# A column mean over 8192 rows: the last row group of the last 64 KB load is summed by TensorE instead of VectorE, and the accumulator is summed ahead of the last two row groups

## The chip, the cores and the metric

The kernel runs on one core of one Trainium2 chip. The metric is the device time of one execution in microseconds (us). Runs of one batch were made on one chip, with the kernel before timed beside them. The "span" is the profiled part of an execution and is some 1.8 us shorter than its time (631.2 us against 633.02 us in the profiled run of the kernel before). In profile lines PE is TensorE's matmuls and PEld its weight loads, DVE is VectorE, ACT ScalarE, POOL GpSimd and SP SyncE; a "q" behind the name is that engine's own queue, issuing a transfer. The "granted clock" is the share of TensorE's full clock that the records of a run show.

## The reference

```
x: 8192 x 8192 float32
out = np.mean(x, axis=0)         # 8192 float32
```

The input is 268.4 MB, so this is a kernel of loads. Row group g is the 128 rows from 128g on, one row for each partition; there are 64 of them, 0 to 63. (In a load of two row groups the rows are dealt out two to a partition, which a sum does not notice.)

## The kernel before

VectorE adds row groups into an accumulator of 128 x 8192, which leaves one row for each partition. TensorE then sums over the partitions, by matmuls with a stationary operand of 1/8192. The sums stand in PSUM tiles: four "banks" and a small one, the "edge". The last two row groups are given to TensorE straight, so that they need no add on VectorE.

```python
def sums(row, blocks, first, last):      # sum over partitions, into PSUM
    for i in blocks:
        if i < NBLK:                     # 15 blocks of 512 columns, four to a bank,
            mm(banks[i // 4], i % 4, row[:, i * F:(i + 1) * F], first, last)   # one column tile each
        else:                            # block 15: four short sums, the "edge"
            for q in range(4):
                c = i * F + q * W
                mm(edge, q, row[:, c:c + W], first, last)
# ... loads of 64 KB (two row groups) or 32 KB (one) per partition; for each row group:
            elif g < G - 3:
                nc.vector.tensor_add(out=acc[:], in0=acc[:], in1=row)
            else:                        # row group 61: in four chunks
                for c in range(0, N, 4 * F):
                    s = slice(c, c + 4 * F)
                    nc.vector.tensor_add(out=acc[:, s], in0=acc[:, s], in1=row[:, s])
# ... row group 62 in one load, row group 63 in pieces of 8, 4, 3 and 1 blocks
    cuts = [(0, 8), (8, 12), (12, 15), (15, 16)]
# ...
    sums(t[:, 0, :], range(NBLK + 1), True, False)       # row group 62
    for b in range(4):
        sums(acc, range(4 * b, 4 * b + 4), False, False) # accumulator
    for lo, hi in cuts:
        sums(t[:, 1, :], range(lo, hi), False, True)     # row group 63
        # for each bank now complete:
        #   nc.scalar.copy(out=r[:32 * n, :], in_=banks[b][:32 * n, :])
        #   nc.scalar.dma_start(out=o, in_=r[0:32 * n:32, :])
        # for the edge: copy by VectorE, store by SyncE
```

The scheduler that places these instructions may move them on an engine where no dependence forbids it.

Of the kernel before, what the change touches and what calls it, by code (L numbers as in the profile page):

```python
# [1 line left out]

# [4 lines left out]


@with_exitstack
def kernel(  # L10
    ctx: ExitStack,
    tc: tile.TileContext,
    x: bass.AP,
    out: bass.AP,
):










    nc = tc.nc
    f32 = mybir.dt.float32
    M, N = x.shape
    P = nc.NUM_PARTITIONS
    F = 512  # L30
    W = F // 4
    NBLK = N // F - 1
    G = M // P

    pairs = ctx.enter_context(tc.tile_pool(name="pairs", bufs=2))
    singles = ctx.enter_context(tc.tile_pool(name="singles", bufs=1))
    sg = ctx.enter_context(tc.tile_pool(name="sg", bufs=1))
    psp = ctx.enter_context(tc.tile_pool(name="psum", bufs=1, space=bass.MemoryType.PSUM))
    resp = ctx.enter_context(tc.tile_pool(name="res", bufs=1))

    acc = sg.tile([P, N], f32, name="acc")
    ones = sg.tile([P, 32], f32, name="ones")
    warm = sg.tile([P, 32], f32, name="warm")
    nc.gpsimd.memset(ones[:], 1.0 / M)  # L44
    nc.scalar.copy(out=warm[:], in_=ones[:])  # L45
    banks = [psp.tile([P, F], f32, name=f"bank{b}") for b in range(4)]
    edge = psp.tile([P, W], f32, name="edge")

    def mm(dst, q, rhs, first, last):
        nc.tensor.matmul(  # L50
            out=dst[32 * q:32 * q + 32, :],
            lhsT=ones[:],
            rhs=rhs,
            start=first,
            stop=last,
            tile_position=(0, 32 * q),
            skip_group_check=True,
        )

    def sums(row, blocks, first, last):  # L60
        for i in blocks:
            if i < NBLK:
                mm(banks[i // 4], i % 4, row[:, i * F:(i + 1) * F], first, last)
            else:
# [4 lines that stand above are left out]
    g = 0  # L69
    k = 0  # L70
    prev = None
    while g < G - 2:
        n = 1 if k % 3 == 2 and g + 2 < G - 2 else 2
        if n == 2:
            t = pairs.tile([P, 2, N], f32, name="pair")
            src = x[g * P:(g + 2) * P, :].rearrange("(p j) c -> p j c", j=2)
            nc.sync.dma_start(out=t[:], in_=src)  # L77
            rows = [t[:, 0, :], t[:, 1, :]]
        else:
            t = singles.tile([P, N], f32, name="single")  # L80
            nc.sync.dma_start(out=t[:], in_=x[g * P:(g + 1) * P, :])
            rows = [t[:]]
        for row in rows:
            if g == 0:
                prev = row
            elif g == 1:
                nc.vector.tensor_add(out=acc[:], in0=prev, in1=row)  # L87
            elif g < G - 3:
                nc.vector.tensor_add(out=acc[:], in0=acc[:], in1=row)  # L89
            else:  # L90
                for c in range(0, N, 4 * F):
                    s = slice(c, c + 4 * F)
                    nc.vector.tensor_add(out=acc[:, s], in0=acc[:, s], in1=row[:, s])  # L93
            g += 1
        k += 1

    t = pairs.tile([P, 2, N], f32, name="pair")
    nc.sync.dma_start(out=t[:, 0, :], in_=x[g * P:(g + 1) * P, :])
    cuts = [(0, 8), (8, 12), (12, 15), (15, 16)]
    for lo, hi in cuts:  # L100
        cs = slice(lo * F, hi * F)
        nc.sync.dma_start(out=t[:, 1, cs], in_=x[(g + 1) * P:(g + 2) * P, cs])
    sums(t[:, 0, :], range(NBLK + 1), True, False)
    for b in range(4):
        sums(acc, range(4 * b, 4 * b + 4), False, False)
    for lo, hi in cuts:
        sums(t[:, 1, :], range(lo, hi), False, True)
        if hi <= NBLK:
            for b in range(lo // 4, (hi + 3) // 4):
                n = min(hi - 4 * b, 4)  # L110
                r = resp.tile([P, F], f32, name=f"r{b}")
                nc.scalar.copy(out=r[:32 * n, :], in_=banks[b][:32 * n, :])  # L112
                o = out[b * 4 * F:(b * 4 + n) * F].rearrange("(q c) -> q c", q=n)
                nc.scalar.dma_start(out=o, in_=r[0:32 * n:32, :])  # L114
        else:
            r = resp.tile([P, W], f32, name="redge")
            nc.vector.tensor_copy(out=r[:], in_=edge[:])  # L117
            o = out[lo * F:hi * F].rearrange("(q c) -> q c", q=4)
            nc.sync.dma_start(out=o, in_=r[0:P:32, :])


# [1 line left out]
_INS = ['x']  # L123
_OUTS = [((8192,), 'float32')]


# [23 lines left out]
```

## Time and profile before

| | kernel before |
|---|---|
| time, median of the first three runs | 633.48 us (633.03 to 633.92) |
| span of the profiled run | 631.2 us |
| load queue's share of the 16 DMA engines | 98.6% |
| VectorE busy | 530.7 us, 84% |
| TensorE, matmuls | 12.9 us, all behind 614.2 us |

Such a table is read from its largest share: loads fill the span, and only what lies behind the last byte can be moved. The prediction shows the lines for that.

### The profile page before, as it was taken

Reading aid. Unit: us, or ns where it says so; the run is one execution under the profiler, and the core shown is the slowest. Engines: PE = TensorE matmul, PEld = TensorE weight load, DVE = VectorE, ACT = ScalarE, POOL = GpSimd, SP = SyncE. Lnnn points to the kernel's source line nnn. Section 1 sums busy time; section 2 is a strip of 40 time slices with the busy share of each in tenths; the row PEclk is TensorE's granted clock in tenths of the full one; section 3 lists DMA queues with packets and bytes.
Section 4 is the critical chain, followed back from the end, with each engine's and each line's share of the span. In section 5 each row is a group of like instructions: output and inputs, shape, how many; then the busy total and the mean of one; then the engine's idle time right before and its main releaser. Section 6 shows DMA issues by size and latency. Waiting matters only on the chain.

```text
span 631.2 us, 470 instructions
## 1 busy us (share of the span) xinstructions
PE 12.9 (2%) x114; PEld 4.9 (1%) x114; DVE 530.7 (84%) x65; ACT 3.7 (1%) x6; POOL 0.3 (0%) x5
## 2 busy tenths in 40 slices
PE   0000000000000000000000000000000000000007
PEld 0000000000000000000000000000000000000002
DVE  0539889889889889889899898898988988988984
ACT  0000000000000000000000000000000000000001
POOL 0000000000000000000000000000000000000000
PEclk9999999999999999999999999999999999999999
DMA  9999999999999999999999999999999999999994
GB/s 399 424 417 455 432 413 451 440 411 461 415 428 436 465 399 465 399 432 432 465 399 465 399 465 399 466 407 457 415 449 428 436 440 424 449 415 457 407 413 189
DMA packets 6090, 268.50 MB, mean 425 GB/s; under 512 B 692, under 2 KB 696, under 8 KB 967
## 3 DMA queue, kind: packets, MB, share of 16 engines
q1 hardware_dynamic: 6056, 268.44, 98.6%
q10 hardware_dynamic: 30, 0.03, 0.0%
q8 instruction: 1, 0.02, 0.0%
q14 instruction: 3, 0.02, 0.0%
HBM read 268.44 MB, written 0.03 MB: 425 GB/s over the span
## 4 chain that ended last, share of the span: by engine, by line
DMA 64%; DVE 33%; PE 2%; issue 0%; ACT 0%; ACTq 0%; SPq 0%; DVEq 0%
DMA pair<-in_x_dram 64%; DVE acc L89 33%; PE bank L50 2%; ACT r L112 0%; ACTq L114 0%; PE edge L50 0%; SPq L77 0%; DVEq L89 0%
## 5 line engine op out<-in xcount | busy, mean ns | idle before, releaser
L89 DVE TENSOR_TENSOR acc<-acc,pair 128x8192 f32<-128x8192 f32 x47 | 408.5, 8692 | 68.5 <-DMA pair<-in_x_dram 67.8
L89 DVE TENSOR_TENSOR acc<-acc,single 128x8192 f32<-128x8192 f32 x12 | 104.3, 8692 | 0.4
L87 DVE TENSOR_TENSOR acc<-pair 128x8192 f32<-128x8192 f32 x1 | 8.7, 8692 | 22.7 <-DMA pair<-in_x_dram 22.7
L50 PE MATMUL bank<-pair,ones 128*32 128x512 f32 x60 | 9.1, 715 | 614.2 <-DMA pair<-in_x_dram 614.2
L93 DVE TENSOR_TENSOR acc<-acc,pair 128x2048 f32<-128x2048 f32 x4 | 8.9, 2287 | 0.0
L50 PEld LDWEIGHTS bank<-pair,ones 128*32 128x32 f32 x60 | 2.8, 127 | 618.7 <-issue 617.9
L112 ACT COPY r<-bank 128x512 f32<-128x512 f32 (+1 forms) x4 | 2.2, 586 | 624.0 <-PE bank L50 623.3
L117 DVE COPY redge<-edge 128x128 f32<-128x128 f32 x1 | 0.3, 292 | 5.1 <-PE bank L50 5.1
L50 PE MATMUL bank<-acc,ones 128*32 128x512 f32 x30 | 3.8, 595 | 0.0
L50 PE MATMUL edge<-pair,ones 128*32 128x128 f32 x16 | 1.6, 276 | 0.0
L50 PEld LDWEIGHTS bank<-acc,ones 128*32 128x32 f32 x30 | 1.4, 109 | 1.5 <-DVE acc L93 0.7
L45 ACT ACT_TABLE_LOAD x1 | 1.3, 1283 | 0.7 <-PEq L134 0.7
L50 PE MATMUL edge<-acc,ones 128*32 128x128 f32 x8 | 0.8, 276 | 0.0
L50 PEld LDWEIGHTS edge<-pair,ones 128*32 128x32 f32 x16 | 0.8, 109 | 1.1 <-issue 1.1
L50 PEld LDWEIGHTS edge<-acc,ones 128*32 128x32 f32 x8 | 0.4, 109 | 0.6 <-issue 0.6
L45 ACT COPY warm<-ones 128x32 f32<-128x32 f32 x1 | 0.2, 218 | 0.0
L44 POOL MEMSET ones<- 128x32 f32 x1 | 0.1, 124 | 0.3 <-POOLq L134 0.3
L134 POOL MEMSET const-bfloat16-1.0<- 128x1 bf16 x1 | 0.1, 101 | 0.0
L134 POOL MEMSET const-uint8-127<- 128x1 uint8 x1 | 0.1, 101 | 0.0
L134 POOL MEMSET const-float32-0.0<- 128x1 f32 x1 | 0.1, 98 | 0.2 <-issue 0.2
L134 POOL MEMSET const-float32-1.0<- 128x1 f32 x1 | 0.1, 98 | 0.0
## 6 DMA issues: line engine op xcount, KB each, us to landing
single<-in_x_dram SPq DMA_DIRECT2D x12, 4096.0 KB, 31.9
pair<-in_x_dram SPq DMA_DIRECT2D x1, 4096.0 KB
pair<-in_x_dram SPq DMA_DIRECT2D x1, 2048.0 KB
pair<-in_x_dram SPq DMA_DIRECT2D x1, 1024.0 KB, 27.8
pair<-in_x_dram SPq DMA_DIRECT2D x1, 768.0 KB, 29.2
pair<-in_x_dram SPq DMA_DIRECT2D x25, 30.9
pair<-in_x_dram SPq DMA_DIRECT2D x1, 256.0 KB, 29.3
out_dram<-r ACTq DMA_DIRECT2D x3, 8.0 KB
```

The source lines that it names most:

```text
L44: nc.gpsimd.memset(ones[:], 1.0 / M)
L45: nc.scalar.copy(out=warm[:], in_=ones[:])
L50: nc.tensor.matmul(out=dst[32 * q:32 * q + 32, :], lhsT=ones[:], rhs=rhs, start=first, stop=last, tile_position=(0, 32 * q), skip_group_ch ...
L87: nc.vector.tensor_add(out=acc[:], in0=prev, in1=row)
L89: nc.vector.tensor_add(out=acc[:], in0=acc[:], in1=row)
L93: nc.vector.tensor_add(out=acc[:, s], in0=acc[:, s], in1=row[:, s])
L112: nc.scalar.copy(out=r[:32 * n, :], in_=banks[b][:32 * n, :])
L117: nc.vector.tensor_copy(out=r[:], in_=edge[:])
L134: nc = _bacc.Bacc("TRN2", target_bir_lowering=False, num_devices=1)
```

## The change

The intent: VectorE is freed of row group 61's four chunked adds, TensorE has that work early, while VectorE still adds row group 60, and the accumulator, which is then ready sooner, is summed before row group 62, so that less is left to sum when row group 63 lands.

```diff
             elif g < G - 3:
                 nc.vector.tensor_add(out=acc[:], in0=acc[:], in1=row)
             else:
-                for c in range(0, N, 4 * F):
-                    s = slice(c, c + 4 * F)
-                    nc.vector.tensor_add(out=acc[:, s], in0=acc[:, s], in1=row[:, s])
+                sums(row, range(NBLK + 1), True, False)
@@
-    sums(t[:, 0, :], range(NBLK + 1), True, False)
-    for b in range(4):
-        sums(acc, range(4 * b, 4 * b + 4), False, False)
+    sums(acc, range(NBLK + 1), False, False)
+    sums(t[:, 0, :], range(NBLK + 1), False, False)
```

## The prediction

> **What bounds the kernel now.** I read the page's totals first, then the chain of waits, then the end of the run in order of time. The totals:
>
> ```profile
> PE 12.9 (2%) x114; PEld 4.9 (1%) x114; DVE 530.7 (84%) x65; ACT 3.7 (1%) x6; POOL 0.3 (0%) x5
> ...
> q1 hardware_dynamic: 6056, 268.44, 98.6%
> HBM read 268.44 MB, written 0.03 MB: 425 GB/s over the span
> ...
> L93 DVE TENSOR_TENSOR acc<-acc,pair 128x2048 f32<-128x2048 f32 x4 | 8.9, 2287 | 0.0
> ```
>
> The load queue keeps the 16 DMA engines busy for 98.6% of the span. VectorE, at 84%, has slack: a pair of row groups takes about 19.5 us to arrive and 2 x 8.69 us to add. So the body, up to the last byte, is bound by the loads, and the change touches no load. Work taken off VectorE is worth nothing by itself. What can be gained lies behind the last byte, and I look for the chain there:
>
> ```profile
> 592.82 21.25 DMA pair<-in_x_dram
> 614.06 0.14 issue
> 614.20 4.59 PE bank L50 x25
> ...
> 619.72 2.74 PE bank L50 x24
> ...
> 623.40 0.91 PE bank L50 x4
> 624.31 0.02 issue
> 624.33 0.59 ACT r L112
> 624.92 0.02 issue
> 624.95 1.11 ACTq L114
> ...
> 627.88 0.58 ACT r L112
> ```
>
> The first column is the start in us. Row group 62 lands at 614.06. From then on TensorE never waits: row group 62, the accumulator, row group 63. Bank 0 is complete at 624.31, and then ScalarE runs its four copies and four store issues one behind another; the span ends at 631.2, 6.87 us after the first copy starts. In the stretches of time the loads die away before that: 0.99 of the DMA engines busy up to 622.5, 0.19 from 622.5 to 624, 0.02 after. By issue start plus time to landing (29.3 us for the 256 KB piece, issued at 594.6) the last piece is there at about 623.9. So TensorE, queued up behind row group 62, makes bank 0 late. It does not wait for data there.
>
> How fast TensorE goes is seen from its weight loads, which keep step with the matmuls:
>
> ```profile
> 615.02 0.22 PEld L50 LDWEIGHTS bank<-pair,ones 128*32 128x32 f32 x4 [0.63 <-issue]
> 615.88 0.22 PEld L50 LDWEIGHTS bank<-pair,ones 128*32 128x32 f32 x4 [0.63 <-issue]
> 616.73 0.22 PEld L50 LDWEIGHTS bank<-pair,ones 128*32 128x32 f32 x4 [0.63 <-issue]
> 617.59 0.15 PEld L50 LDWEIGHTS bank<-pair,ones 128*32 128x32 f32 x4 [0.63 <-issue]
> 618.03 0.13 PEld L50 LDWEIGHTS bank<-pair,ones 128*32 128x32 f32 x3 [0.29 <-issue]
> 618.46 0.13 PEld L50 LDWEIGHTS bank<-pair,ones 128*32 128x32 f32 x3 [0.30 <-issue]
> ```
>
> Four loads make half a bank. Up to 617.59 half a bank takes 0.855 us, from there 0.43 us. TensorE starts at half speed, though the page's clock row shows nothing of it.
>
> **What the Trainium skill says.** "TensorE: Matmul & The Clock Gate", Part 1, gives a cold clock of half the rate, left after about 3.4 us of activity, in windows that run free of the kernel, and taken up again after an idle window of about the same length. The trace agrees: 614.17 to 617.59 is 3.42 us at half pace. When it falls back this trace does not show within the work. "FP8 and Floating Point Precision", section TensorE Precision Notes, has true fp32 as four passes through the array, and the first page's Part 3 lets four column tiles run at once. Together, at its 2.4 GHz, a bank of four 512-column blocks is 4 x 512 / 2.4 = 853 ns; the trace has 2 x 0.43 us. "DMA: Bandwidth & Descriptors", Specifications, puts the fabric's ceiling at 435 GB/s; the kernel gets 425, so nothing is left in the body.
>
> **The change part by part.** A row group is 15 blocks in four banks plus four short edge sums. Warm it takes 3.67 us (the accumulator's first matmul starts at 619.35, row group 63's at 623.02). From cold it takes 5.2 us (614.17 to 619.35).
>
> 1. Removed: four chunked adds on VectorE, 8.9 us, from 613.17 to 622.07. VectorE's last big add then ends at 613.13 (604.44 + 8.69). It frees nothing in the loads. But the accumulator, whose last chunk was ready only at 622.07, is now whole at 613.13.
>
> 2. Added: row group 61 on TensorE. It lands with row group 60, whose add starts at 604.44, so TensorE starts at about 604.5, cold, and is done between 609.7 and, had it stayed cold all the way, 611.7. It lies wholly beside the add of row group 60, which lasts to 613.13: on the path it costs 0. It also pays for the slow start. TensorE then idles 1.5 to 3.4 us; the windows run on across this gap, and for nearly every position of a 3.4 us window there is some work in each window. I take the clock as still full at 613.2.
>
> 3. Moved: the accumulator first, 613.18 to 616.85 (3.67 us warm). Row group 62 has landed by then (614.06): 616.85 to 620.52. Row group 63 follows. Its first 2 MB come 4.9 us after row group 62, at about 619.0 (2.1 MB at 426 GB/s), so they are there too.
>
> 4. Bank 0 was ready 1.3 us after row group 63 began (623.02 to 624.33, copy started). The same from 620.52 gives 621.83. That is 2.5 us earlier.
>
> 5. Does the rest follow? The pieces of row group 63 land at about 621.5 (issued 593.7, plus 27.8), 623.3 (594.1 + 29.2) and 623.9. Bank 3's blocks are in the third piece: 623.3 + 0.14 to get going + 1.3 = 624.75. The fourth copy, shifted with the chain, starts at 627.88 - 2.5 = 625.4. So data is there with 0.65 us to spare, and ScalarE's serial chain still sets the end. The edge needs the fourth piece: 623.9 + 0.14, behind bank 3 on TensorE, some 0.7 us for matmuls, 0.29 for the copy, a store issue by 625.1 to 625.7: off the path.
>
> Sum: the end moves from 631.2 to 628.7 in the span, -2.5 us, and the time from 633.48 to 631.0. I put the centre at 631.1 for the mix with the rivals below.
>
> **The rivals.** (a) VectorE as bound. At 84% busy, taking 8.9 of its 530.7 us could be thought worth 1.4% of the time. Against it: VectorE idles for a DMA before almost every pair (67.8 us in the groups). This rival would give about 624.6. I give it 1%.
> (b) The clock falls back in the gap. If a gap of 3.4 us or a nearly empty window is enough, the accumulator starts cold again, takes 5.2 us in place of 3.67, and all behind it moves by some 1.6 us: bank 0 at 623.4, a gain of 0.9 us, 632.6. For it: the gap is as long as the skill's window. Against: the window would have to fall exactly on it. 15%.
> (c) The last landing takes over. If the last pieces come later than my sums (a store issued while loads run shares the engines; the fourth copy has 0.65 us of slack only), the gain shrinks to 1.5 or 2 us: 631.5 to 632. 20%.
> (d) The new matmuls slow the add or the loads beside them. Against: with TensorE at work from 614 to 619 the loads ran at 413 GB/s, against 410 from 609 to 614, and the four chunk adds took 2.28 us each, whether beside matmuls or not. It would cost under 0.5 us.
> (e) TensorE was held by VectorE at the end before: the last chunk was done at 622.07 and TensorE's loads waited 0.7 us for it. Without that wait its work may pack a bit closer than my 3.67. This is worth at most 0.3 us more, and the third piece caps it.
>
> **Range and chances.** The three runs of before spread by 0.9 us (633.03 to 633.92), from the loads, so a median can move by 0.4 us either way without the change. The main case, 631.0 give or take 0.4, has about 60%; (b) and (c) pull upward to 632.6, (e) downward to 630.6. Range 630.3 to 632.6. A 2% change would be 12.7 us. All work behind the last byte and its wait is 631.2 - 623.9 = 7.3 us, so faster by over 2% is out of reach unless the loads change: 1%. Slower by over 2% would need 12.7 us from matmuls that stand beside an add: 0.5%.
>
> **What would show it.** Right: VectorE ends at about 613.1 but for the edge copy; TensorE works from 604.5 to 610 or 611.5, pauses, starts the accumulator at 613.2 with weight loads 0.43 us apart per half bank, row group 62 at 616.9, row group 63 at 620.5; the first ScalarE copy starts near 621.8, and 6.9 us later the span ends; the load queue's bytes and rate are as before. The chain of waits then leads from ScalarE through TensorE back to the add of row group 60, no longer to row group 62's landing. Half-bank steps of 0.855 us behind 613.2 would show (b); a wait of TensorE for the last pieces with ScalarE idle between copies shows (c); a longer add at 604.4 shows (d). The prediction is wrong if the whole time leaves the range, or if the span is shorter because loads end sooner.

## More of the kernel before

The columns are start, duration, engine, line, operation and tiles; "ACTq" is ScalarE's own queue issuing a store.

```profile
626.10 1.07 ACT L112 COPY r<-bank 128x512 f32<-128x512 f32 x2 [1.18 <-PE bank L50]
626.72 1.13 ACTq L114 DMA_DIRECT2D out_dram<-r  x2
627.88 0.58 ACT L112 COPY r<-bank 96x512 f32<-96x512 f32 x1 [0.71 <-ACT r L112]
```

Copies 1 and 2 stand next to each other, and the two stores follow together. A store's issue overlaps the second copy here (626.72 is ahead of 627.17, where the copies end).

## The result, and the profile after

The changed kernel took 631.68 us (median of four runs, 630.75 to 632.36), the kernel before beside it 633.70 us (633.03 to 633.92). The ratio is 0.9969, with a 95% interval of 0.995 to 0.9987. A ratio here is the mean time of one kernel's runs over that of the other's of the same rounds, so it is not quite the ratio of the medians. The gain is about 2.0 us, or 0.3%; the time is within the predicted range. No single run took 631.68 us: the median lies midway between two runs near 630.9 and two near 632.35 us, so it depends on how many runs fall into either group.

The totals of the page of the changed kernel:

```profile
PE 19.3 (3%) x152; PEld 6.6 (1%) x152; DVE 521.8 (83%) x61; ACT 3.8 (1%) x6; POOL 0.3 (0%) x5
...
q1 hardware_dynamic: 6056, 268.44, 98.6%
```

VectorE lost its 8.9 us (530.7 to 521.8), TensorE gained 6.4 us, and the load queue is as it was. The chain of waits in order of time:

```profile
604.13 8.70 DVE acc L89
612.84 0.04 issue
612.88 4.59 PE bank L50 x25
...
618.40 2.72 PE bank L50 x24
...
622.06 0.91 PE bank L50 x4
622.97 0.02 issue
623.00 0.59 ACT r L109
...
627.11 0.58 ACT r L109
```

The chain now comes from the add of row group 60, no longer from row group 62's landing. Compare the stretches of TensorE with those of before: the accumulator's first 25 matmuls took 4.59 us, as long as row group 62's from cold did before, and the next row's took 2.72 us. So the accumulator was summed at a slow start too. The weight loads, with the matmuls on either side of the pause, in order of time, show it:

```profile
610.23 0.40 PE L50 MATMUL edge<-pair,ones 128*32 128x128 f32 x6
...
612.88 0.20 PEld L50 LDWEIGHTS bank<-acc,ones 128*32 128x32 f32 x8 [2.52 <-DVE acc L89]
612.88 4.88 PE L50 MATMUL bank<-acc,ones 128*32 128x512 f32 x27 [2.25 <-DVE acc L89]
613.74 0.20 PEld L50 LDWEIGHTS bank<-acc,ones 128*32 128x32 f32 x4 [0.66 <-issue]
...
616.30 0.12 PEld L50 LDWEIGHTS bank<-acc,ones 128*32 128x32 f32 x4 [0.66 <-issue]
616.73 0.12 PEld L50 LDWEIGHTS bank<-acc,ones 128*32 128x32 f32 x3 [0.31 <-issue]
```

Row group 61 was done at 610.63. After a pause of 2.25 us the half banks again come 0.855 us apart, until 616.30. The stretches of time have the granted clock to it (third from the last column; the engines' busy times stand before it):

```profile
609.00:614.00 5.00, 2.75 (x26) 0.88 (x23) 3.83 (x1) 0.00 (x0) 0.00 (x0) 0.89 0.93 397
614.00:619.00 5.00, 5.00 (x43) 1.55 (x39) 0.00 (x0) 0.00 (x0) 0.00 (x0) 0.77 0.96 408
```

Half speed for 1.1 us of the first stretch (5 x 0.11 x 2) puts the fall at 612.9, and for 2.3 us of the second puts the rise at 616.3. The clock had come up at full, and fell back just as the accumulator's sums began. This is the prediction's rival (b), in the run that was profiled.

The four timed runs do not agree with one another as executions usually do: 632.35 and 632.36 us with a mean granted clock of 0.997, 631.02 and 630.75 us with 1.0. A stretch of 3.4 us at half speed makes 0.997 of a span of 630 us (3.4 x 0.5 / 630 = 0.0027), so the two groups look like runs in which the clock fell back and runs in which it didn't. The trace shown is of the slow group, and so is the only other trace of this kernel that was taken, so the fast group has no trace of its own.

ScalarE's end differs too:

```profile
624.76 0.58 ACT L109 COPY r<-bank 128x512 f32<-128x512 f32 x1 [1.18 <-PE bank L50]
625.38 0.51 ACTq L111 DMA_DIRECT2D out_dram<-r  x1
625.94 0.58 ACT L109 COPY r<-bank 128x512 f32<-128x512 f32 x1 [0.59 <-PE bank L50]
```

Copy and store now go by turns, so that each copy waits for the issue of the store before it. From the first copy to the fourth it is 4.11 us (623.00 to 627.11), against 3.55 us before (624.33 to 627.88). The source lines of these copies and stores are the same in both kernels, so the order was made by the scheduler.

### The profile page after: what moved, and what is told of

It is laid out like the page before. It is cut to its first block, busy times and chain, and to the rows that moved or that the text cites. A ratio compares the mean times of both kernels' runs of the same rounds, so it can differ in the third digit from the quotient of the medians.

```text
span 630.5 us, 542 instructions
## 1 busy us (share of the span) xinstructions
PE 19.3 (3%) x152; PEld 6.6 (1%) x152; DVE 521.8 (83%) x61; ACT 3.8 (1%) x6; POOL 0.3 (0%) x5
## 3 DMA queue, kind: packets, MB, share of 16 engines
q1 hardware_dynamic: 6056, 268.44, 98.6%
## 4 chain that ended last, share of the span: by engine, by line
DMA 64%; DVE 33%; PE 2%; ACT 0%; ACTq 0%; issue 0%; DVEq 0%
DMA pair<-in_x_dram 64%; DVE acc L89 32%; PE bank L50 2%; DVE acc L87 1%; ACT r L109 0%; ACTq L111 0%; PE edge L50 0%; DVEq L89 0%
## 5 line engine op out<-in xcount | busy, mean ns | idle before, releaser
L50 PE MATMUL bank<-pair,ones 128*32 128x512 f32 x90 | 13.7, 720 | 604.2 <-DMA pair<-in_x_dram 604.2
L50 PEld LDWEIGHTS bank<-pair,ones 128*32 128x32 f32 x90 | 4.5, 129 | 610.8 <-issue 608.9
L50 PE MATMUL bank<-acc,ones 128*32 128x512 f32 x30 | 5.3, 837 | 2.3 <-DVE acc L89 2.3
```

The lines of the kernel that those rows point to most:

```text
L50: nc.tensor.matmul(out=dst[32 * q:32 * q + 32, :], lhsT=ones[:], rhs=rhs, start=first, stop=last, tile_position=(0, 32 * q), skip_group_ch ...
```

## The experiments

Two theories stand against each other for the spread and for the size of the gain. One is the clock gate: what counts is whether TensorE's clock is up when the sums behind 612.9 us begin. The other is that the loads vary, or that VectorE's freed time is what pays. Ten runs follow, each of five timed executions, in three batches, each batch on another chip; the kernel before ran nine times beside each batch (medians 633.59, 634.01 and 633.60 us; all 27 runs between 632.93 and 634.44).

| run | median, us | range, us | before in its batch | ratio |
|---|---|---|---|---|
| after_again | 631.27 | 630.94 to 632.75 | 633.59 | 0.9967 |
| e1_filler_in_gap | 631.15 | 630.88 to 631.29 | 633.59 | 0.9958 |
| e2_before_warm | 633.15 | 632.82 to 633.48 | 633.59 | 0.9991 |
| e3_row61_left_out | 633.33 | 632.80 to 633.79 | 633.59 | 0.9993 |
| e4_part1_alone | 632.83 | 631.15 to 633.06 | 634.01 | 0.998 |
| e5_part2_alone | 636.77 | 636.47 to 636.97 | 634.01 | 1.0047 |
| e7_scalar_order_of_before | 630.65 | 630.50 to 630.78 | 634.01 | 0.9951 |
| e8_stores_from_sync | 630.26 | 630.17 to 630.37 | 634.01 | 0.9945 |
| e6_rows60_61_on_tensor | 630.47 | 630.25 to 630.68 | 633.60 | 0.9952 |
| e9_both | 630.31 | 630.13 to 630.53 | 633.60 | 0.9949 |

**after_again.** No edit.

> The changed kernel once more, with more rounds. Theory (the clock gate): its runs fall into two groups, one near 630.9 us with a mean granted clock of 1.0 and one near 632.35 us with 0.997, according to whether TensorE's clock falls back in the pause ahead of the accumulator's sums. Rival (the loads vary): one cloud between 630.7 and 632.4, with no tie between the time and the clock.

Measured: 632.75 and 632.33 us with a clock of 0.997, 630.94, 631.27 and 630.99 us with 1.0, 1.0 and 0.999. With the four runs of the result that is nine runs: four at 632.33 to 632.75, all at 0.997, and five at 630.75 to 631.27, all at 0.999 or 1.0. Nothing lies between. The two groups are there, and the clock tells them apart. (Means of 0.998 and 0.999 in fast runs come, where a trace shows it, from a fall behind the last matmul: in e6's trace the last matmul ends at 625.04, the clock falls at 626.39, and the mean is 0.998. The records begin with the first rise, so a slow start ahead of it does not lower the mean.)

**e1_filler_in_gap.** TensorE is given something to do in the pause:

```diff
+    junk = psp.tile([P, F], f32, name="junk")
+    def fill(row, blocks):
+        for i in blocks:
+            mm(junk, i % 4, row[:, i * F:(i + 1) * F], True, True)
@@
                 sums(row, range(NBLK + 1), True, False)
+                fill(row, range(12))
```

> The changed kernel with 12 blocks of matmuls more (3 banks' worth, 2.6 us at full clock) on row group 61's data into a bank that nobody reads, so that TensorE has no pause ahead of the accumulator. Theory (clock gate): the clock no longer falls back, every run is near 630.9 us or up to 0.3 us later, the slow group is gone, ratio to before about 0.996, and the scatter shrinks under 0.5 us. Rival (the loads vary): the same two groups as the changed kernel, or one cloud as wide. Rival (more TensorE work costs time): 2 us slower than the changed kernel.

All five runs are in the fast group, 0.4 us apart. Nine and five runs are few, but with four slow of nine, five fast ones in a row would be a chance of about 5% (5/9 to the fifth power). The trace shows the mechanism directly:

```profile
610.32 2.76 PE L51 MATMUL junk<-pair,ones 128*32 128x512 f32 x23
613.55 3.21 PE L51 MATMUL bank<-acc,ones 128*32 128x512 f32 x27 [0.47 <-DVE acc L94]
```

The accumulator's 27 matmuls take 3.21 us here against 4.88 us in the trace of the changed kernel. Bank 0 is copied from 621.98; that is 17.2 us after the add of row group 60 began (604.80), against 19.9 us in the kernel before (624.33 less 604.44) and 18.9 us in the changed kernel's trace (623.00 less 604.13). More matmuls made the kernel no slower.

**e2_before_warm.** The kernel before with filler from 604.2 on (`fill` and `junk` as in e1):

```diff
                     nc.vector.tensor_add(out=acc[:, s], in0=acc[:, s], in1=row[:, s])
+                fill(row, range(16))
+                fill(row, range(14))
```

> The kernel before with 30 blocks of filler matmuls from 604.2 on, so that TensorE's clock is up when row group 62 lands at 614.1. Theory: row group 62 is then summed by about 617.9, but the accumulator's last chunk is added only at 622.07, so the sums of it still end near 623.0 and the time is that of the fastest runs of before, 633.0 us, with less scatter (before: 633.0 to 633.9); ratio 0.999. Rival (TensorE's slow start alone held the kernel before, VectorE's chunks nothing): 1.7 us off, near 631.5 to 632.

The expectation held: 633.15 us, as the best runs of before, with a spread of 0.66 us in place of the 1.2 us of before in the same batch. TensorE's matmuls in order of time:

```profile
617.48 1.89 PE L51 MATMUL bank<-acc,ones 128*32 128x512 f32 x15
619.62 1.07 PE L51 MATMUL bank<-acc,ones 128*32 128x512 f32 x8 [0.25 <-DVE acc L98]
621.83 0.63 PE L51 MATMUL bank<-acc,ones 128*32 128x512 f32 x3 [1.14 <-DVE acc L98]
```

With a full clock TensorE waits for VectorE's chunks (0.25 and 1.14 us), and row group 63 still begins only at 622.7. So two limits lay side by side in the kernel before: TensorE's cold start, and the last chunked add at 622.07. To take away the cold start alone gives little (0.44 us between the medians); e3 and e4 take away the chunks.

**e3_row61_left_out.** The sums are taken out, and the accumulator's first matmuls start the groups:

```diff
-                sums(row, range(NBLK + 1), True, False)
+                pass
@@
-    sums(acc, range(NBLK + 1), False, False)
+    sums(acc, range(NBLK + 1), True, False)
```

The result is wrong (relative error 0.125); the loads and all the rest are as in the changed kernel.

> The changed kernel without row group 61's sums: a wrong result on purpose (one row group of 64 is missing). TensorE then idles until 612.9 and starts the accumulator from cold in every run. Theory: as the slow group of the changed kernel, near 632.3 us, or up to 1 us more where the clock comes up later, and no run near 630.9. Rival (row group 61's sums on TensorE cost something on the path): faster than the changed kernel's fast group, under 630.7 us.

633.33 us: slower than even the slow group, at the upper edge of what was expected with three runs a little over it, and almost the time of the kernel before. Without row group 61's matmuls ahead of it TensorE is cold for 4.0 us in this trace (613.07 to 617.1, by the pace of its loads):

```profile
613.07 5.18 PE L50 MATMUL bank<-acc,ones 128*32 128x512 f32 x27 [613.07 <-DVE acc L89]
```

The gain of the freed VectorE and the new order together is 0.26 us between the medians, not clear of the noise (the interval of the ratio is 0.9981 to 1.0006). It is also an undercount: in e3 ScalarE's copies and stores go by turns, as in the changed kernel, and e7 below puts that at 0.5 us; without it some 0.8 us would be left, as an estimate from these two numbers. Row group 61's sums cost nothing that shows on the path, and their warming is the larger part of the gain: 633.33 less the fast group's 631.0 is 2.3 us, with ScalarE's order the same in both.

**e4_part1_alone.** Row group 61 on TensorE, with the sums of the last lines in the old order:

```diff
-    sums(acc, range(NBLK + 1), False, False)
-    sums(t[:, 0, :], range(NBLK + 1), False, False)
+    sums(t[:, 0, :], range(NBLK + 1), False, False)
+    sums(acc, range(NBLK + 1), False, False)
```

> Only the first part of the change: row group 61 on TensorE, but the accumulator summed behind row group 62 as in the kernel before. TensorE then pauses some 3.5 us until row group 62 lands. Theory (the clock drops after a window with little work, and the pause here is longer): cold in nearly every run, so row group 62 takes 5.2 us or more again, and nothing is gained although VectorE is done 8.9 us earlier: 633.2 to 634.2 us, ratio 0.999 to 1.001. Rival (it is VectorE's chunks that held the end): 631.5 us, ratio 0.997.

This was a miss in part. Four of five runs were cold (0.997), as expected, but at 632.8 to 633.1 us they are about 1.2 us below the kernel before of their batch; and one run, at a clock of 1.0, took 631.15 us. The trace is of a cold run:

```profile
614.04 4.81 PE L50 MATMUL bank<-pair,ones 128*32 128x512 f32 x27 [4.47 <-DMA pair<-in_x_dram]
```

The cold stretch was 3.3 us (614.04 to about 617.3), and nothing waited for a chunked add behind it. A kernel that starts cold, as the one before or e3, can be cold for longer (4.0 us in e3). This difference would account for the gain that was not expected, but it was read from single traces, not tried. ScalarE's order in e4's trace is that of the kernel before, two and two, so that the 1.2 us holds no loss from the order by turns.

**e5_part2_alone.** Row group 61 stays on VectorE in chunks, and the accumulator goes first. The matmuls were also pinned in the written order (that part of the edit is not shown here).

```diff
-    sums(t[:, 0, :], range(NBLK + 1), True, False)
-    for b in range(4):
-        sums(acc, range(4 * b, 4 * b + 4), False, False)
+    sums(acc, range(NBLK + 1), True, False)
+    sums(t[:, 0, :], range(NBLK + 1), False, False)
```

> Only the second part: row group 61 stays on VectorE in four chunks, but TensorE sums the accumulator ahead of row group 62 (its matmuls pinned in the written order). Theory: the last chunk is there at 622.07, so row group 62 (3.7 us warm, 5.2 cold) is summed only from 623.0, row group 63 from 626.7 to 628.2, and the span ends 7.5 us after bank 0's copy starts at 628 to 629.5: 637.4 to 639 us, ratio 1.006 to 1.009. Rival (the order of the sums alone gives the gain): 631 to 632 us.

636.77 us, 2.8 us slower than before: the direction as expected, the size 0.6 us under the range. Row group 62's sums began at 623.2, behind the last chunk, and at full clock; and ScalarE's order was the better one (bank 0's copy at 628.18, the end at 635.1, 6.9 us), where 7.5 us had been reckoned. The new order pays only with part 1.

**e7_scalar_order_of_before.** The filler version with ScalarE's instructions pinned to copy 0, store 0, copies 1 and 2, stores 1 and 2, copy 3, store 3:

```diff
+    held = []
@@
-                nc.scalar.copy(out=r[:32 * n, :], in_=banks[b][:32 * n, :])
+                if b == 2:
+                    late, held = held, []
+                tc.keep_in_program_order(nc.scalar.copy(out=r[:32 * n, :], in_=banks[b][:32 * n, :]))
                 o = out[b * 4 * F:(b * 4 + n) * F].rearrange("(q c) -> q c", q=n)
-                nc.scalar.dma_start(out=o, in_=r[0:32 * n:32, :])
+                held = [(o, r[0:32 * n:32, :])]
+                if b == 2:
+                    held = late + held
+                if b != 1:
+                    for o, rs in held:
+                        tc.keep_in_program_order(nc.scalar.dma_start(out=o, in_=rs))
+                    held = []
```

> The filler version (TensorE kept busy in the gap) with ScalarE's tail in the order of the kernel before: copy 0, store 0, copies 1 and 2, stores 1 and 2, copy 3, store 3; the changed kernel has copy and store by turns. Theory: from the first copy's start to the end of the span it is 6.9 us in the order of before and 7.5 us by turns, so this run is 0.6 us faster than the filler version: 630.5 us. Rival (data for bank 3, not ScalarE, sets the end): no difference, 631.1 us.

630.65 us against 631.15 us. The batches differ, so the spans are better compared by their own marks: from the first copy to the end it is 7.0 us (621.90 to 628.87), against 7.5 us in e1 (621.98 to 629.51). The order of the copies and stores is worth 0.5 us.

**e8_stores_from_sync.** The filler version, stores by another queue:

```diff
-                nc.scalar.dma_start(out=o, in_=r[0:32 * n:32, :])
+                nc.sync.dma_start(out=o, in_=r[0:32 * n:32, :])
@@
-            nc.sync.dma_start(out=o, in_=r[0:P:32, :])
+            nc.scalar.dma_start(out=o, in_=r[0:P:32, :])
```

> The filler version with the four result stores issued by SyncE instead of ScalarE (the small edge store goes to ScalarE). Theory: ScalarE's serial chain of copies and store issues set the end; without the issues the copies follow the data, the fourth waits only for the third piece of row group 63, and the end moves 1.0 us ahead: 630.1 us. Rival (the last landing and the store's own flight set the end): 631.1 us as the filler version.

630.26 us, 0.9 us below e1, with a spread of 0.2 us. (The two stand in different batches; against its own kernel before, the ratio is 0.9945 here and 0.9958 in e1.) Its chain of waits from the last loads on, but for short issue times, is this:

```profile
594.18 29.70 DMA pair<-in_x_dram
...
623.93 0.95 PE bank L51 x4
624.88 0.14 PE edge L51
...
625.04 0.58 ACT r L115
```

It goes back to the last pieces of row group 63, on which TensorE goes to work at 623.93, and no longer to the accumulator.

**e6_rows60_61_on_tensor.** No filler: TensorE takes both row groups of the last 64 KB load, and the accumulator is summed ahead of them.

```diff
-            elif g < G - 3:
+            elif g < G - 4:
@@
+                if g == G - 4:
+                    sums(acc, range(NBLK + 1), True, False)
-                sums(row, range(NBLK + 1), True, False)
+                sums(row, range(NBLK + 1), False, False)
@@
-    sums(acc, range(NBLK + 1), False, False)
     sums(t[:, 0, :], range(NBLK + 1), False, False)
```

> The changed kernel carried one step further: TensorE takes both row groups of the last 64 KB load, 60 and 61, and the accumulator (done by VectorE at about 601) is summed ahead of both. No filler. Theory: TensorE is warm by about 606 and has no pause over a microsecond until row group 62 lands, so there is no slow group; row group 63's first piece is waited for, and the end is set by the third piece's landing (about 623.8), then 1.1 us of sums, a copy, a store and its flight: 630.2 us, scatter under 0.4. Rival (the added 7.3 us of TensorE work delays row group 62): 631 to 633 us.

630.47 us, with no slow run. The chain of waits of this run ends so:

```profile
593.97 29.75 DMA pair<-in_x_dram
623.72 0.04 issue
623.76 1.09 PE bank L50 x6
624.85 0.02 issue
624.88 0.58 ACT r L110
```

The third piece's landing is the bound. TensorE waits for data at each of row group 63's three large pieces, and its pause before them is under a microsecond. This beats both kernels with a correct result and no wasted matmul: 3.1 us under the kernel before.

**e9_both.** e6 with e8's edit.

> The previous run's kernel with the result stores issued by SyncE. Theory: with the third piece's landing as the bound, ScalarE's store issues are hidden in the previous run already, so this one is within 0.2 us of it and of the filler version with stores from SyncE: 630.2 us. Rival (ScalarE's chain still matters): 0.5 us or more faster than the previous run.

630.31 us, 0.16 us below e6, as expected where the last landing is the bound.

**Where the clock falls.** The clock records of the traces give the moments at which it was raised and lowered. They lie multiples of 3.41 us apart within a run. Read against TensorE's busy time in each such window, they give shares that none of the runs was made for, so this is an observation and not a test. The two windows of the changed kernel around the fall:

```profile
609.47:612.88 3.41, 1.16 (x18) 0.28 (x9) 3.36 (x1) 0.00 (x0) 0.00 (x0) 1.00 0.91 389
612.88:616.29 3.41, 3.41 (x16) 0.79 (x20) 0.00 (x0) 0.00 (x0) 0.00 (x0) 0.50 1.03 437
```

TensorE is busy for 1.16 of 3.41 us in the first, and the clock is at half in the second. More windows around a pause or a start:

| in the window | clock at its end | runs |
|---|---|---|
| 0%, 34%, 41% busy | fell | e4, the changed kernel, after_again |
| 49%, 66%, 73% busy | stayed up | e5, e2, e4 |
| 55%, 70% busy | stayed down | the changed kernel, after_again |
| 78%, 79%, 91% busy | was raised | e4, e2, e5 |

The other windows of the twelve traces, up to the end of each kernel, agree: with the clock up, windows of 41% or less let it fall and windows of 47% or more kept it; with the clock down, windows of up to 70% left it there and windows from 78% on raised it. The ends of matmuls are modelled in a profile, so the shares are rough. Where the windows lie against the kernel's work differs from trace to trace; that this splits the runs of the changed kernel is likely but not shown, since none of its fast runs has a trace.

## Why the prediction was right or wrong

The predicted time was 631.1 us, in a range of 630.3 to 632.6; measured was 631.68 us. Faster by over 2% did not come, as said.

- The bound was read rightly: the load queue is unchanged at 98.6%, and the 8.9 us taken off VectorE did not come off the time (rival (a) fell; e3, with all of them gone, gained 0.26 us, or some 0.8 us but for ScalarE's new order).
- Step 2's cost was right: row group 61 from cold ended at 610.63, within the 609.7 to 611.7 given, beside the add and off the path. Its last sentence is the step that failed: "I take the clock as still full at 613.2", because "for nearly every position of a 3.4 us window there is some work in each window". Some work is not enough. Windows with 34% and 41% of work let the clock fall, though the pauses in them were only 2.25 and 2.00 us long. So rival (b), put at 15%, was the case in four of nine runs. Its number was right, 632.6 predicted and 632.33 to 632.75 measured, but partly by luck, as the points on step 5 and on the total show.
- Step 4, bank 0 2.5 us earlier, was right where the clock stays up: 2.7 us in e1, which stands in for the fast group. In the profiled slow run it was 1.0 us, near the 0.9 us of rival (b).
- Step 5 failed in a term of its sum: the chain behind bank 0 was shifted as a whole with its 6.87 us, but the scheduler had changed ScalarE's order, and it takes 7.5 us (623.00 to 630.54). The prediction read the copies and stores as running "one behind another", missed the overlap in the trace of before, and did not ask in which order the changed kernel would have them.
- In the total the misses were made up by luck. The stages were read from the profiled run of before, the fastest of its four (633.02 us; its clock rose after 3.4 us), but the 2.5 us were taken off the median, 633.48 us. From the profiled run, 633.02 - 2.7 + 0.7 (bank 0 earlier and ScalarE longer, both as in e1) gives 631.0, the fast group's median; the prediction's 633.48 - 2.5 = 631.0 is the same number with two errors of about half a microsecond against each other. The same holds for rival (b).
- Rival (e) gave VectorE's last chunk 0.3 us at most, and the text above it has TensorE "never" waiting, though (e) itself names a wait of 0.7 us. In the kernel before it was nearly as strong a limit as the cold start: with the clock up, TensorE waits for it and the time stays (e2).
- Rival (c), a later landing, did not come up in the changed kernel's traces. It is the bound in e6, e8 and e9. Rival (d) was not seen: the add beside row group 61's sums took 8.69 us, as all others.

The spread of the kernel before was put down to the loads. The runs speak against it: e1, e6, e7, e8 and e9, in which TensorE's clock is up ahead of the sums that count, spread by 0.2 to 0.45 us, with the same loads; e3, which starts from cold, spread by 1.0 us. That the length of the cold start makes the spread of the kernel before fits this, but no trace of one of its slower runs was taken.

## What to carry to other kernels

In a tail of a few microseconds behind the last load, ask first whether TensorE's clock is up when it matters; useful work put just ahead can be worth more through the clock than through its own sum. Undo each part of a change alone: here one part gave 1.2 us, the other cost 2.8, and both together gave 2.0 to 2.3. When two kernels differ, compare the order of instructions on every engine, also on those whose source lines did not change.

## What the Trainium skill lacked or had wrong

- "TensorE: Matmul & The Clock Gate", Part 1, has the clock fall after an idle window. Here windows with up to 41% of work let it fall, with pauses of only 2.25 and 2.00 us, and windows with 47% and more did not. The window length of 3.4 us agrees with these runs.
- The same section has it raised after a busy window. Here up to 70% of a window did not raise it, 78% did. The page gives no share for either.
- On none of the pages read: a kernel's first store from ScalarE took 1.11 us to issue, the later ones of the same size 0.51 and 0.52 us (the changed kernel's trace: 623.61 to 624.72, then 625.38 and 626.55); and where copies and store issues go by turns on ScalarE instead of two and two, a tail of four pairs took 0.5 us longer (e1 against e7).
